# An encoder trunk on one core: the first outputs of a head two projections ahead of the second

## The chip, the cores and the metric

The kernel runs on one core of one Trainium2 chip. The metric is the time of one execution on the device in microseconds (us); lower is better. The time of the kernel before is the median of three runs.

## The reference, cut to what matters

One layer is applied to a prompt (1024 tokens) and to a sample (512 tokens), width 1024, all in float32. The token mixer that matters here is a gated linear recurrence with 8 heads of width 128 that runs forwards and backwards:

```
proj = rmsnorm(x) @ w_in                 # q, f_fw, f_bw, i, z_a, ... , g_a, g_b: 11 blocks of 1024
f = lb + (1 - lb) * sigmoid(f_raw);  k = (1 - lb) * sigmoid(-f_raw);  v = i
S_t = diag(f_t) S_{t-1} + k_t v_t^T;  o_t = S_t^T q_t      # forwards, and the same backwards
o = o_forward + o_backward
o = o * rsqrt(mean(o * o) + eps) * hnorm_g                 # per head
p_a = (o * silu(z_a)) @ w_a
```

A second branch (a short convolution with gates), the merge of both branches, one more projection and a last norm follow.

## The kernel before, in words

The program runs in stages. First the prompt's tokens are normed and projected (values, then all other blocks of the prompt, by a Strassen-like scheme that writes them to memory). Then comes the stage that the change touches: the recurrence of all 8 heads for prompt and sample, interleaved with the plain projections of the sample. After it the output projections follow.

In this stage each head has three blocks of 512 tokens: the prompt's blocks 0 and 1 (together one group) and the sample's one block (a group of its own). A block has four chunks of 128 tokens. The loop over `order` makes one turn for each block, 24 and one more, and a turn works on several blocks at once, in a software pipeline:

- `near_scores(prev)` (L450) and `scores(prev)` (L463): small products of 32 or 64 columns (L447, L481) of the decayed keys and queries, into the banks `sc`; ScalarE and VectorE copy them together into the tile `pt`.
- `transpose_keys(prev)` (L490) and `contributions(prev)` (L501): the keys are transposed (L496) and multiplied with the values (L509), and ScalarE copies the products to `us` (L510).
- `decays(cur)` (L409): for the next block, seven levels of decayed keys and queries, on VectorE (`K` L433, `Q` L413 and L434), ScalarE (copies into `cat`, L431 and L432) and GpSimd (products of the forget gates `T`, L421).
- `states(g)` (L513): when all blocks of a group are done, a chain of VectorE operations over the chunks turns the contributions into states, in place in `us` (L518): 12 for a prompt group, 4 for a sample group.
- `outputs(g, b)` (L521): for one block of a group, the products of scores with values and of queries with states (L533: 11 for a prompt block, 10 for a sample block; the trace counts each of these float32 products twice, as 22 and 20), all into the single bank `o`. Then ScalarE squares them and reads the sums (L537, four pairs), VectorE adds eps (L538), GpSimd raises to the power -1/2 (L98), and ScalarE copies the scaled products to the tile `oz` (L541, four). Only then is the bank free.
- `finish(g)` (L543): transposes of `oz` for all blocks of a group (L547), a product with the gate (L548), a store.
- `unit()`: one projection of the sample, 24 products of 512 columns (L94; 96 for the two wide ones, L87). Three units a turn. Their weights are loaded and split (L63 on ScalarE, L64 on VectorE) three units ahead.

Since a prompt group is complete after its block 1, the turns of a head differ. In the turn whose `prev` is the sample block (turn 1 below), `to_output` is the prompt group and nothing is to be finished. In the next turn (turn 2; `prev` is block 0 of the next head) `to_output` is the sample group, which has one block only, so its second `outputs` call finds no block, and `to_finish` is the prompt group. In turn 3 (`prev` is block 1) nothing is to be output, and the sample group is finished.

What sets the order: TensorE executes in the order in which the program is written (a manual schedule, L381). All other engines, and the queue of transfers, get their order from a planner, which simulates the program and prefers what stands earlier in it; once planned, each engine works strictly in that order. Buffers that matter: bank `o` one, banks `u` two, `sc` two, the projections' `pp` three (eight in all); `Q`, `K`, `F`, `pt` and `oz` three tiles each, `cat` eight, `us` and the values one for each kind of group.

The body of `outputs` after its products, for one block:

```python
                for c in range(CPB):
                    A.activation(oz[:, c, :], p[:, c, :], AF.Square, accum_out=ss[:, c:c + 1])
                V.tensor_scalar(ss, ss, 1.0 / P, EPS, op0=ALU.mult, op1=ALU.add)
                r = rsqrt(gp, ss, "o")
                for c in range(CPB):
                    A.activation(oz[:, c, :], p[:, c, :], AF.Copy, scale=r[:, c:c + 1])
```

The loop itself stands whole in the section on the change. After the loop come `unit()`, `outputs` of the last sample group, `finish`, `unit()` and `finish`; these stay as they are.

Of the kernel before, what the change touches and what calls it, by code (L numbers as in the profile page):

```python
# [43 lines left out]
def trunk_kernel(ctx: ExitStack, tc: tile.TileContext, xs, w, outs, masks_d, ident_d):  # L44
# [51 lines left out]
    def rsqrt(pool, t, name):  # L96
        r = pool.tile(list(t.shape), F32, name=f"rs_{name}")
        G.tensor_tensor(r, t, neghalf[:, :t.shape[-1]], op=ALU.pow)  # L98
        return r
# [275 lines left out]
    with outer:  # L375
# [7 lines left out]
        def gtile(name, shape, bufs=1):  # L383
            return gp.tile([P, *shape], F32, name=name, bufs=bufs)

        def bank(name, bufs, shape=(CPB, P)):
            return ps.tile([P, *shape], F32, name=name, bufs=bufs)
# [12 lines left out]
        def loaded(group, b):  # L400

            k = Block(group, b)
            src = fkq_d[k.tb][group.h]
            load(k.F, src[:, 0:2, :])
            load(k.K, src[:, 2:4, :])
            load(k.q, src[:, 4, :])
            return k

        def decays(k):  # L409

            F, K, q = k.F, k.K, k.q
            k.Q = Q = gtile("Q", [2, TB], 3)
            V.scalar_tensor_tensor(Q, ap(q, 0, [[0, 2], [1, TB]]), float(P) ** -0.5, F, op0=ALU.mult, op1=ALU.mult)  # L413
            k.kd = gtile("kd", [TB], 2)
            V.tensor_tensor(k.kd, K[:, 0, :], K[:, 1, :], op=ALU.add)

            Ts = [(F, TB)]
            while Ts[-1][1] > CPB:
                t, m = Ts[-1]
                tn = gtile(f"T{TB * 2 // m}", [2, m // 2], 1 if m // 2 > CPB else 4)  # L420
                G.tensor_tensor(tn, ap(t, 0, [[m, 2], [2, m // 2]]), ap(t, 1, [[m, 2], [2, m // 2]]), op=ALU.mult)  # L421
                Ts.append((tn, m // 2))
            k.total = Ts[-1][0]
            k.cats = []
            for hs, (t, m) in zip(LEVELS, Ts):
                nb = TB // (2 * hs)
                cat = gtile("cat", [2, TB], 8)
                k.cats.append(cat)
                kall = ap(K, TB, [[2 * hs, nb], [hs - TB, 2], [1, hs]])
                qall = ap(Q, 0, [[2 * hs, nb], [hs + TB, 2], [1, hs]])  # L430
                A.copy(ap(cat, 0, [[2 * hs, nb], [hs, 2], [1, hs]]), kall)  # L431
                A.copy(ap(cat, TB, [[2 * hs, nb], [hs, 2], [1, hs]]), qall)  # L432
                V.tensor_tensor(kall, kall, ap(t, m + 1, [[2, nb], [-m - 1, 2], [0, hs]]), op=ALU.mult)  # L433
                V.tensor_tensor(qall, qall, ap(t, 1, [[2, nb], [m - 1, 2], [0, hs]]), op=ALU.mult)  # L434
# [15 lines left out]
        def near_scores(k):  # L450

            k.sc = []
            score_products(k, range(4))
            k.near = near = gtile("near", [CPB, Q32])
            A.activation(near, k.sc[0][:, 0, :, :], AF.Copy, scale=float(P) ** -0.5)
            for li in range(1, 4):
                pick(k, li)
# [5 lines left out]
        def scores(k):  # L463

            score_products(k, range(4, 7))
            for li in range(4, 6):
                pick(k, li)
            k.pt = pt = gtile("pt", [CPB, P], 3)
            for s in range(4):
                r, x = slice(s * Q32, (s + 1) * Q32), slice((s ^ 1) * Q32, ((s ^ 1) + 1) * Q32)  # L470
                A.copy(pt[r, :, x], k.sc[1][r, 2, :, :])
                A.copy(pt[r, :, r], k.near[r, :, :])
            far_scores(k)
# [11 lines left out]
        def chunks_for(k, d):  # L485

            cs = [c for c in range(CPB) if (k.b * CPB + c < k.g.n - 1 if d else k.b * CPB + c > 0)]
            return cs, slice(cs[0], cs[-1] + 1)

        def transpose_keys(k):  # L490
            k.kT = []
            for d in (1, 0):
                cs, span = chunks_for(k, d)
                p = bank("u", 2)
                for c in cs:
                    T.transpose(p[:, c, :], k.K[:, d, c * P:(c + 1) * P], ident)  # L496
                kT = gtile("kT", [CPB, P], 2)
                A.copy(kT[:, span, :], p[:, span, :])
                k.kT.append(kT)
# [13 lines left out]
        def states(g):  # L513
            us = g.us
            for d, cs in ((1, range(1, g.n - 1)), (0, range(g.n - 2, 0, -1))):
                for c in cs:
                    t = g.done[c // CPB].total[:, d, c % CPB:c % CPB + 1]
                    V.scalar_tensor_tensor(us[:, d, c, :], us[:, d, c + (1 - 2 * d), :], t, us[:, d, c, :],  # L518
                                           op0=ALU.mult, op1=ALU.add)

        def outputs(g, b):  # L521
            for k in g.done[b:b + 1]:
                p = bank("o", 1)
                for c in range(CPB):
                    n = k.b * CPB + c
                    cols = slice(c * P, (c + 1) * P)
                    mms = [(k.pt[:, c, :], g.v[:, n, :])]
                    if n > 0:
                        mms.append((k.Q[:, 1, cols], g.us[:, 1, n - 1, :]))
                    if n < g.n - 1:  # L530
                        mms.append((k.Q[:, 0, cols], g.us[:, 0, n + 1, :]))
                    for m, (l, r) in enumerate(mms):
                        T.matmul(p[:, c, :], l, r, start=m == 0, stop=m == len(mms) - 1)  # L533
                k.oz = oz = gtile("oz", [CPB, P], 3)
                ss = gtile("sso", [CPB], 2)
# [7 lines that stand above are left out]
        def finish(g):  # L543
            for k in g.done:
                p = bank("u", 2)
                for c in range(CPB):
                    T.transpose(p[:, c, :], k.oz[:, c, :], ident)  # L547
                V.tensor_tensor(k.oz, p, g.zg[:, k.b * TB:(k.b + 1) * TB].rearrange("p (c t) -> p c t", c=CPB), op=ALU.mult)  # L548
                store(oz_d[k.tb][g.h], k.oz.rearrange("p c t -> p (c t)"))
# [84 lines left out]
        def prepare(n):  # L634
            while todo and len(ready) < n:
                p, m = todo.pop(0)
                ready.append((m, p()))

        def unit():
            prepare(AHEAD + 1)  # L640
            if ready:
                m, x = ready.pop(0)
                m(x)
# [4 lines left out]
        def values(g):  # L648
            g.v = gtile(f"v{g.n}", [g.n, P])
            src = v_d[0:8] if g.n == 8 else v_d[8:12]  # L650
            load(g.v, src[:, :, g.h * P:(g.h + 1) * P].rearrange("c p e -> p c e"))
# [9 lines left out]
        prev, to_output, to_finish = None, None, None  # L661
        for i in range(len(order) + 1):
            cur = None
            if i < len(order):
                cur = nxt if order[i][0] else sample[order[i][1]]
                if i + 1 < len(order) and order[i + 1][0]:
                    nxt = loaded(*order[i + 1])
            if prev:
                near_scores(prev)
                transpose_keys(prev)  # L670
            if cur:
                decays(cur)
                if cur.b == 0:
                    values(cur.g)
                    if cur.g.n == 8:
                        cur.g.zg = gtile("zgp", [2 * TB])
                        load(cur.g.zg, zg_d[cur.g.h])
            unit()
            if prev:
                scores(prev)  # L680
                contributions(prev)
            if to_output:
                outputs(to_output, 0)
            unit()
            if to_output:
                outputs(to_output, 1)
            if to_finish:
                finish(to_finish)
            unit()
            to_finish, to_output = to_output, None  # L690
            if prev and len(prev.g.done) == len(prev.g.tbs):
                to_output = prev.g
                states(prev.g)
            prev = cur
# [280 lines left out]
```

## Time and profile before

| what | value |
| --- | --- |
| three runs | 1972.35, 1977.19, 1985.93 us; median 1977.19 |
| the profiled execution | 1982.88 us |
| its span, first to last instruction | 1981.1 us |
| mean granted clock of TensorE | 0.988 of 2.4 GHz |
| busy: TensorE, VectorE, ScalarE, GpSimd | 1940.3, 1476.4, 981.5, 170.2 us |
| stage of the recurrence, in the span | about 900 to 1580 us |

The profile holds one execution. Times in it count from the span's start. A timeline row gives the start, the duration, the engine, the line of the program, the operation, what it writes and reads, how many instructions are merged, and in brackets how long the engine sat idle before it and what it waited for. Matmuls are pipelined: the next starts before the modelled end of the one before, so lengths of a stretch of TensorE's work are best taken from start to start.

### The profile page before, as it was taken

How to read it: one execution, taken by the hardware profiler on the slowest of the kernel's cores; microseconds unless marked ns; L12 is line 12 of the kernel's file. 1: busy time of each engine (PE TensorE's matmuls, PEld its weight loads, DVE VectorE, ACT ScalarE, POOL GpSimd, SP SyncE). 2: the span in 40 equal slices, each digit the busy share in tenths (PEclk: the TensorE clock that was granted, in tenths of full speed). 3: DMA queues.
4: the chain of work that ended last, by engine and by line, in shares of the span. 5: the costliest groups of instructions: out<-in, count | busy, mean ns of one | idle time of the engine just before them, and what ended most of it. 6: DMA issues, size and time to landing. Idle time of an engine off the chain costs nothing.

```text
span 1981.1 us, 37160 instructions
## 1 busy us (share of the span) xinstructions
PE 1940.3 (98%) x14820; PEld 1633.4 (82%) x14820; DVE 1476.4 (75%) x2369; ACT 981.5 (50%) x1956; POOL 170.2 (9%) x220
## 2 busy tenths in 40 slices
PE   9999999999999999998999999999999999999998
PEld 8988888888888888886888888888888887888786
DVE  6558686878676777776688878879788378765687
ACT  6433333343424333345677877877877443332332
POOL 1000000000000000003121322322212000000000
PEclk8999999999999999998999999999999999999999
DMA  7433333333324242435443534434333497798653
GB/s 214 146 108 103 115 96 107 102 120 97 120 88 131 77 138 75 128 113 184 146 124 118 161 112 128 142 106 156 110 120 104 143 308 254 241 313 278 214 186 107
DMA packets 313757, 288.85 MB, mean 146 GB/s; under 512 B 19184, under 2 KB 252912, under 8 KB 313584
## 3 DMA queue, kind: packets, MB, share of 16 engines
q1 hardware_dynamic: 313584, 286.49, 45.8%
q8 instruction: 116, 1.90, 0.4%
q14 instruction: 57, 0.47, 0.1%
HBM read 208.84 MB, written 77.59 MB: 145 GB/s over the span
## 4 chain that ended last, share of the span: by engine, by line
PE 77%; issue 9%; DVE 5%; DMA 5%; ACT 3%; POOL 1%; SPq 0%; DVEq 0%; POOLq 0%; ACTq 0%
PE pp L309 38%; PE pp L94 16%; PE pw L781 9%; PE pp L215 5%; PE o L533 2%; PE pp L87 2%; PE sc L447 2%; DMA io<-in_w_o 1%; PE u L509 1%; DVE Q L434 1%; DVE K L433 1%; ACT cat L431 1%; DVE w_l L64 1%; DMA w_raw<-in_w_b 1%; PE tp L177 1%
## 5 line engine op out<-in xcount | busy, mean ns | idle before, releaser
L309 PE MATMUL pp<-s_h,w_h 128*128 128x512 f32 x1120 | 435.9, 389 | 1.2 <-ACT w_h L63 1.2
L309 PE MATMUL pp<-s_l,w_h 128*128 128x512 f32 x1120 | 435.7, 389 | 0.0
L309 PE MATMUL pp<-s_h,w_l 128*128 128x512 f32 x1120 | 435.7, 389 | 0.0
L63 ACT ACTIVATE w_h<-w_raw 128x1024 fp32r<-128x1024 f32 (+1 forms) x250 | 209.6, 838 | 323.4 <-PE pp L309 137.8
L94 PE MATMUL pp<-s_h,w_h 128*128 128x512 f32 x896 | 356.5, 398 | 0.0
L94 PE MATMUL pp<-s_h,w_l 128*128 128x512 f32 x896 | 350.0, 391 | 1.5 <-DVE w_l L64 1.5
L94 PE MATMUL pp<-s_l,w_h 128*128 128x512 f32 x896 | 350.0, 391 | 0.2 <-DVE s_l L64 0.2
L64 DVE TENSOR_TENSOR w_l<-w_raw,w_h 128x1024 fp32r<-128x1024 f32 (+1 forms) x250 | 238.4, 954 | 101.0 <-ACT w_h L63 99.4
L314 DVE TENSOR_TENSOR tmp<-pp,tmp 128x512 f32<-128x512 f32 x240 | 165.3, 689 | 156.1 <-PE pp L309 156.1
L309 PEld LDWEIGHTS pp<-s_h,w_h 128*128 128x128 f32 x1120 | 210.2, 188 | 45.3 <-ACT w_h L63 1.8
L309 PEld LDWEIGHTS pp<-s_l,w_h 128*128 128x128 f32 x1120 | 210.2, 188 | 43.6
L309 PEld LDWEIGHTS pp<-s_h,w_l 128*128 128x128 f32 x1120 | 210.2, 188 | 43.6
L63 ACT ACTIVATE w_h<-w_S 128x512 fp32r<-128x512 f32 x160 | 101.0, 632 | 263.4 <-PE pp L309 263.3
L94 PEld LDWEIGHTS pp<-s_h,w_l 128*128 128x128 f32 x896 | 168.6, 188 | 38.3 <-DVE w_l L64 2.3
L94 PEld LDWEIGHTS pp<-s_l,w_h 128*128 128x128 f32 x896 | 168.9, 189 | 34.1 <-DVE s_l L64 1.0
L94 PEld LDWEIGHTS pp<-s_h,w_h 128*128 128x128 f32 x896 | 169.2, 189 | 33.0 <-ACT w_h L63 0.3
L431 ACT COPY cat<-K 128x512 f32<-128x512 f32 x168 | 111.6, 668 | 36.8 <-DVE K L433 35.4
L433 DVE TENSOR_TENSOR K<-K,T 128x512 f32<-128x512 f32 x144 | 110.1, 764 | 18.7 <-ACT cat L431 17.4
L432 ACT COPY cat<-Q 128x512 f32<-128x512 f32 x168 | 111.4, 668 | 19.4 <-DVE Q L434 10.8
L434 DVE TENSOR_TENSOR Q<-Q,T 128x512 f32<-128x512 f32 x144 | 104.0, 722 | 16.2 <-ACT cat L432 15.5
L781 PE MATMUL pw<-s_h,w_h 128*128 128x512 f32 x280 | 110.6, 395 | 2.5 <-ACT w_h L63 2.5
L781 PE MATMUL pw<-s_h,w_l 128*128 128x512 f32 x280 | 110.5, 395 | 1.1 <-DVE w_l L64 1.1
(178 smaller groups left out, 2961.5 us busy)
## 6 DMA issues: line engine op xcount, KB each, us to landing
w_raw<-in_w_in SPq DMA_DIRECT2D x166, 512.0 KB, 4.4
fkq_d<-sg SPq DMA_DIRECT2D x48, 256.0 KB, 2.3
io<-cz_p SPq DMA_DIRECT2D x20, 512.0 KB, 5.4
fkq_d<-sk SPq DMA_DIRECT2D x32, 256.0 KB, 2.1
F<-fkq_d SPq DMA_DIRECT2D x16, 512.0 KB, 3.7
K<-fkq_d SPq DMA_DIRECT2D x16, 512.0 KB, 6.5
w_raw<-in_w_b SPq DMA_DIRECT2D x16, 512.0 KB, 4.8
w_raw<-in_w_a SPq DMA_DIRECT2D x16, 512.0 KB, 6.1
```

Source lines behind the costliest of these rows:

```text
L63: A.activation(hi, src, AF.Copy)
L64: V.tensor_tensor(lo, src, hi.bitcast(F32), op=ALU.subtract)
L87: T.matmul(out, lhs(k, a), parts[k // 2][b][:, k % 2, :], start=k == 0 and n == 0, stop=k == KT - 1 and n == 2)
L94: T.matmul(out, whl[a][:, k, :], rhs(k, b), start=k == 0 and n == 0, stop=k == KT - 1 and n == 2)
L215: T.matmul(pp, B[f"B{k // 4 + 1}{t + 1}"][a][:, k % 4, c * P:(c + 1) * P], parts[k][b], start=k == 0 and m == 0, stop=k == KT - 1 and m == 2)
L309: T.matmul(bank, hl[x][:, k, :], B[b][y][:, k, :], start=k == 0 and i == 0, stop=k == 3 and i == 2)
L314: V.tensor_tensor(out, p, t, op=ALU.add)
L431: A.copy(ap(cat, 0, [[2 * hs, nb], [hs, 2], [1, hs]]), kall)
L432: A.copy(ap(cat, TB, [[2 * hs, nb], [hs, 2], [1, hs]]), qall)
L433: V.tensor_tensor(kall, kall, ap(t, m + 1, [[2, nb], [-m - 1, 2], [0, hs]]), op=ALU.mult)
L434: V.tensor_tensor(qall, qall, ap(t, 1, [[2, nb], [m - 1, 2], [0, hs]]), op=ALU.mult)
L781: T.matmul(bank, hl[x][:, c:c + P], O[n][y][:, k, :], start=k == 0 and i == 0, stop=k == 3 and i == 2)
```

## The change

`outputs(to_output, 0)` moves from behind `contributions(prev)` to a place directly behind `transpose_keys(prev)`, ahead of `decays(cur)` and of the first of the turn's three units. `finish(to_finish)` changes places with `outputs(to_output, 1)`. Nothing else changes. The loop with the diff:

```diff
         for i in range(len(order) + 1):
             cur = None
             if i < len(order):
                 cur = nxt if order[i][0] else sample[order[i][1]]
                 if i + 1 < len(order) and order[i + 1][0]:
                     nxt = loaded(*order[i + 1])
             if prev:
                 near_scores(prev)
                 transpose_keys(prev)
+            if to_output:
+                outputs(to_output, 0)
             if cur:
                 decays(cur)
                 if cur.b == 0:
                     values(cur.g)
                     if cur.g.n == 8:
                         cur.g.zg = gtile("zgp", [2 * TB])
                         load(cur.g.zg, zg_d[cur.g.h])
             unit()
             if prev:
                 scores(prev)
                 contributions(prev)
-            if to_output:
-                outputs(to_output, 0)
             unit()
+            if to_finish:
+                finish(to_finish)
             if to_output:
                 outputs(to_output, 1)
-            if to_finish:
-                finish(to_finish)
             unit()
             to_finish, to_output = to_output, None
             if prev and len(prev.g.done) == len(prev.g.tbs):
                 to_output = prev.g
                 states(prev.g)
             prev = cur
```

## Rows read from the trace of the kernel before

**Rows 1.** Table of engines of the page: busy us, share of span, instructions.

```profile
PE 1940.3 (98%) x14820; PEld 1633.4 (82%) x14820; DVE 1476.4 (75%) x2369; ACT 981.5 (50%) x1956; POOL 170.2 (9%) x220
```

**Rows 2.** Busy time by stretch (busy us and instructions of each engine), 1200 to 1300 us.

```profile
1200.00:1300.00 100.00, 97.99 (x1417) 82.87 (x1416) 86.50 (x145) 78.55 (x179) 25.39 (x32) 1.00 0.45 138
```

**Rows 3.** Waits of TensorE, 900 to 1580 us: total us, times, longest.

```profile
PE o L533 <- ACT oz L541: 14.1, 7, 2.1
PE u L496 <- DVE K L433: 4.8, 1, 4.8
```

**Rows 4.** Timeline of TensorE, turn 1 of the second head.

```profile
1072.17 0.48 PE L94 MATMUL pp<-s_h,w_h 128*128 128x512 f32 x1
...
1080.89 0.39 PE L533 MATMUL o<-v,pt 128*128 128x128 f32 x2
...
1083.27 0.48 PE L94 MATMUL pp<-s_h,w_h 128*128 128x512 f32 x1
...
1090.94 0.49 PE L533 MATMUL o<-v,pt 128*128 128x128 f32 x2 [1.94 <-ACT oz L541]
...
1094.47 0.77 PE L94 MATMUL pp<-s_h,w_h 128*128 128x512 f32 x1
...
1100.68 0.46 PE L447 MATMUL sc<-q,kd 128*32 128x32 f32 x32
```

**Rows 5.** Timeline of ScalarE, turn 1 of the second head; last row: the fourth.

```profile
1074.86 0.62 ACT L431 COPY cat<-K 128x512 f32<-128x512 f32 x1 [1.45 <-DVE K L433]
...
1085.80 0.27 ACT L537 ACTIVATE oz<-o 128x128 f32<-128x128 f32 x1
...
1089.75 1.14 ACT L541 ACTIVATE oz<-o,rs_o 128x128 f32<-128x128 f32 x4 [0.43 <-POOL rs_o L98]
...
1255.17 1.14 ACT L541 ACTIVATE oz<-o,rs_o 128x128 f32<-128x128 f32 x4 [1.88 <-POOL rs_o L98]
```

**Rows 6.** Timeline of TensorE, turn 1 of the fourth and of the last head.

```profile
1239.68 0.48 PE L94 MATMUL pp<-s_h,w_h 128*128 128x512 f32 x1
...
1247.40 0.49 PE L533 MATMUL o<-v,pt 128*128 128x128 f32 x2 [2.01 <-ACT oz L541]
...
1249.88 0.47 PE L94 MATMUL pp<-s_h,w_h 128*128 128x512 f32 x1
...
1255.54 0.46 PE L447 MATMUL sc<-q,kd 128*32 128x32 f32 x32
...
1257.56 0.48 PE L94 MATMUL pp<-s_h,w_h 128*128 128x512 f32 x1
...
1548.63 0.48 PE L94 MATMUL pp<-s_h,w_h 128*128 128x512 f32 x1
...
1554.19 0.38 PE L533 MATMUL o<-v,pt 128*128 128x128 f32 x2
```

**Rows 7.** Stretches of 10 us; the third number from the end is the granted clock.

```profile
1010.00:1020.00 10.00, 7.92 (x40) 6.93 (x39) 7.08 (x13) 7.03 (x20) 3.97 (x6) 0.83 0.32 100
...
1240.00:1250.00 10.00, 7.99 (x47) 6.73 (x46) 6.84 (x10) 8.53 (x25) 2.66 (x3) 1.00 0.17 52
...
1400.00:1410.00 10.00, 8.36 (x41) 7.53 (x42) 7.50 (x11) 6.59 (x21) 5.10 (x7) 0.83 0.55 157
...
1550.00:1560.00 10.00, 10.00 (x57) 8.67 (x56) 1.77 (x4) 4.65 (x20) 2.01 (x2) 1.00 0.26 80
```

**Rows 8.** Timeline of VectorE, second head.

```profile
1068.79 1.13 DVE L518 SCALAR_TENSOR_TENSOR us<-us,T 128x128 f32<-128x128 f32 x3
...
1077.03 0.69 DVE L433 TENSOR_TENSOR K<-K,T 128x512 f32<-128x512 f32 x1 [0.76 <-ACT cat L431]
...
1083.73 1.22 DVE L413 SCALAR_TENSOR_TENSOR Q<-q,F 128x1024 f32<-128x1024 f32 x1
```

**Rows 9.** Timeline of GpSimd, turn 1 of the second head: the two powers.

```profile
1088.71 1.01 POOL L98 TENSOR_TENSOR rs_o<-sso,neghalf 128x4 f32<-128x4 f32 x1 [24.88 <-DVE sso L538]
...
1097.05 1.91 POOL L98 TENSOR_TENSOR rs_o<-sso,neghalf 128x4 f32<-128x4 f32 x1
```

## The prediction

> **What bounds the kernel now.** I read the table of engines first: TensorE is busy for 98% of the span [rows 1], and in the stage of small products a stretch of 100 us shows it at 98.0 while VectorE stands at 86.5 and ScalarE at 78.6 [rows 2]. So TensorE's own stream sets the time, and a change is worth what it takes out of that stream's gaps. The waits of TensorE in this stage come next [rows 3]. Almost all of them have one form: the products of `outputs` (L533) wait for the scaling copies of ScalarE (L541), 7 times, 14.1 us in total, never over 2.1 us. The only other wait of any size comes once, at the start of the stage, and the change does not touch it.
>
> The timeline of TensorE in the second head shows which `outputs` waits [rows 4]. In turn 1, block 0's products start at 1080.89, one projection starts at 1083.27, and block 1's products start only at 1090.94, after 1.94 us of idle. There is one bank `o`. Block 1 may not write it before ScalarE has read block 0 out of it twice, with VectorE's small operation and GpSimd's power between, and one projection is too short a cover. The ScalarE rows of the same turn show the chain: block 0's squares begin at 1085.80, more than 2 us after the products ended, because copies of the scores stand before them in ScalarE's queue, and the last scaling copy ends at 1089.75 + 1.14 = 1090.89, 0.05 before the products of block 1 [rows 5].
>
> **The stall, and what follows it.** A projection without a wait behind it takes 1554.19 - 1548.63 = 5.56 us from its start to that of the products; that is the last head, where no decays compete and no idle stands [rows 6]. In the second head it takes 1090.94 - 1083.27 = 7.67 [rows 4], in the fourth 1247.40 - 1239.68 = 7.72 [rows 6]. One stall so costs 2.11 to 2.16 us, and seven at 2.16 are 15.1 us. (The 14.1 of rows 3 count idle from modelled ends, which lie a little late.)
>
> Second, the clock. Around the stalls the stretches of 10 us show a mean granted clock of 0.83, the first at 1010 to 1020 and the last at 1400 to 1410, five such in all; at the other two stalls it stays at 1.00, as at 1240 to 1250 [rows 7]. So the clock falls to its lower level (1.2 instead of 2.4 GHz) for a while after five of seven stalls, and nowhere else from 1000 to 1580. Its price, by rows: in the fourth head, at full clock, block 1's products and the projection behind them take 1255.54 - 1247.40 = 8.14 us [rows 6]; in the second they take 1100.68 - 1090.94 = 9.74 [rows 4]. That is 1.60 us, times five is 8.0 us.
>
> Here a rule can be weighed. The Trainium skill, "TensorE: Matmul & The Clock Gate", section "Why this matters for your kernels", advises against idle gaps of TensorE that are clearly longer than these 2 us, as what brings the lower clock. Rows 7 with rows 3 disagree as far as they go: five falls, each directly behind one of these gaps. By the page's advice the falls would have another cause and would stay, and the sum would hold the stalls alone, 15.1 us.
>
> **The change part by part.** *The outputs of block 0 go ahead.* No instruction is added or removed. In turn 1, block 0's 22 products move from behind `contributions` to a place directly behind the key transposes, so two projections and two groups of small products lie between block 0 and block 1 instead of one projection. Block 0's chain needs 7.67 us from the end of its products to the free bank [rows 4]. The new cover is at least the two projections, 2 x 5.56 = 11.1 us. The stall of block 1 goes whole.
>
> What the moved products now need earlier: the states of the prompt head (L518), block 0's copied scores, Q, and the bank. The last three state operations start at 1068.79 and take 1.13 us, so they end at 1069.92 [rows 8]; the products' new place is where the projection starts now, 1072.17 [rows 4]. The margin is 2.25 us where it was 10.97 us. The margin is there, and the states stand before turn 1's work in program order, so I take 0 as the cost. The bounds: nothing if the order of VectorE stays; if the last three state operations fall behind the work that VectorE does next, up to the K operation that ends at 1077.03 + 0.69 = 1077.72, the wait is 1077.72 - 1072.17 = 5.6 us a head.
>
> What is queued behind the moved work on the other engines: ScalarE gets the four squares, four accumulator reads and four scaling copies while it has holes (in the second head it waits 1.45 us before the copy of K at 1074.86 [rows 5]). Behind them stand cat copies of the next block and the splits of weights, which are prepared three projections ahead. GpSimd is idle for 24.88 us before block 0's power now [rows 9], so the power finds it free earlier. No DMA moves with `outputs`; the stores belong to `finish`.
>
> A gain without a direct price: the first operation on the next block's Q starts at 1083.73 [rows 8], directly after block 0's products [rows 4], since Q has three buffers and block 0's products free one. Freed 8.7 us earlier, the Q chain can spread over the projections; TensorE does not wait for it now, so I book 0.
>
> *The sample's outputs* (one block) move in turn 2 in the same way, and this is where the bank wait could go next: block 1's products, then one projection, then the near scores and transposes, then these. From the projection's start to the new place are 1257.56 - 1249.88 = 7.68 us [rows 6]. Block 1's chain in this head ends at 1255.17 + 1.14 = 1256.31 [rows 5], 1.25 us in time. Even if it took as long as block 0's chain, 7.67 us, it would just do. So again 0. Nothing can be won below that, since no wait stands there now [rows 3]; as the bound above I take a whole GpSimd power in its slower form, 1.91 us [rows 9], seven times 13.4 us.
>
> *`finish` ahead of the second `outputs`.* In turn 1 nothing waits to be finished (the turn before has no outputs), and in turn 2 the sample group has no second block, so `outputs(…, 1)` issues nothing. The two calls never both issue work in one turn; exchanging them changes nothing, cost 0.
>
> *The last head* has no stall now [rows 6], so it gives nothing.
>
> The sum: 15.1 + 8.0 = 23.1 us. The profiled execution took 1982.88 us for a span of 1981.1; it would take 1959.8. It is 5.7 us above the median of the runs shown, 1977.19, and I have no reason to scale the gain, so the forecast for the median is 1977.2 - 23.1 = 1954.1 us.
>
> **The rivals.**
>
> (a) The bank wait moves to the sample's outputs. For it: the margin is 1.25 us in the fourth head [rows 5, 6], the order of ScalarE will be planned anew, and the second of two powers is the slow one (1.91) [rows 9]. Against: with Q done earlier ScalarE has less to do at that point. A wait of 1.5 us a head gives back 10.5: 1964.6.
>
> (b) The clock falls stay, for another cause than the gaps: only 15.1 is won, 1962.1. Against: the last head has no gap at block 1's products, and the clock stays at 1.00 there, 1550 to 1560 [rows 6, 7]. (The page named above would have it so.)
>
> (c) VectorE or ScalarE becomes the bound. Block 1's products start at 1090.94 in the second head and at 1247.40 in the fourth [rows 4, 6], so a head takes 78.2 us; VectorE works 86.5% of it [rows 2], and shortened by 3.3 us it would work 90%. Against: one engine at 90% with room in its queue still keeps up. If it gives back two thirds: 1969.5.
>
> (d) Slower: the states come late. In turn 1 VectorE's queue is written out by the planner; if the last state operations are placed behind the next block's first K operations, TensorE waits 5.6 us a head right behind the transposes [rows 8]; seven are 39 us, and the falls of the clock stay: 1977.2 - 15.1 + 39 = 2001. It decides for slower once the states are later by 2.25 us of margin and about 2.2 more. Against: in program order the states stand before all of turn 1's work, and their last operations ran before the next block's K [rows 8].
>
> **How the numbers follow.** The forecast 0.62, (a) 0.18, (b) 0.08, (c) 0.06, (d) 0.06. A measurement of this kernel can tell about 1% from no change, here 19.8 us. The forecast's own range is 1948 to 1961: between three and seven falls of the clock (4.8 to 11.2 us in place of 8.0) and some 4 us for the median of three runs that lie 13.6 us apart. Some of it, and (a), (b) and (c), fall short of 1%. Faster by over 1%: 0.57; within: 0.37; slower: 0.06. The range of 1945 to 1968 leaves out (d), most of (c) and the tails.
>
> **What would show it.** Right: no wait of L533 for L541 in TensorE's waits; granted clock 1.00 from 1000 on; in turn 1 the order transposes, products, projection; Q's first operation some 8 us earlier against the near scores. Step by step wrong: a wait of L533 for L518 (d), a wait of L533 for L541 in turn 2 (a), 0.83 without a gap before it (b), waits of projections for the splits L63 or L64, or of scores for the cat copies (c). A median above 1968 or below 1945 makes the prediction wrong.

## The result, and the profile after

The changed kernel takes 1957.64 us (median of 4 runs, 1954.35 to 1960.89); the kernel before 1977.63 (4 runs). The ratio is 0.9895 with a 95% interval of 0.9871 to 0.9919, so 20.0 us by the medians, and 16 to 25.5 by the interval. The forecast was 1954.1 with a gain of 23.1; range and sign hold, and the gain lies inside the interval. The profiled execution took 1960.89 us against 1982.88.

The waits of TensorE in the stage, as in [rows 3]:

```profile
PE u L496 <- DVE K L433: 4.3, 1, 4.3
PE o L533 <- ACT oz L541: 1.8, 3, 1.0
PE pp L87 <- DVE w_l L64: 1.3, 1, 1.3
PE pp L87 <- ACT w_h L63: 1.3, 1, 1.3
PE o L533 <- DVE us L518: 1.3, 1, 1.3
```

The row that carried 14.1 us in 7 waits holds 1.8 in 3, and these stand at another place, as will be seen. A wait for the states (L518) has come in, once.

Turn 1 and the start of turn 2 of the second head on TensorE, beside [rows 4]:

```profile
1071.57 0.39 PE L533 MATMUL o<-v,pt 128*128 128x128 f32 x2
...
1073.94 0.48 PE L94 MATMUL pp<-s_h,w_h 128*128 128x512 f32 x1
...
1082.57 0.47 PE L94 MATMUL pp<-s_h,w_h 128*128 128x512 f32 x1
...
1088.13 0.38 PE L533 MATMUL o<-v,pt 128*128 128x128 f32 x2
...
1096.17 0.46 PE L447 MATMUL sc<-q,kd 128*32 128x32 f32 x32
...
1098.44 0.49 PE L533 MATMUL o<-v,pt 128*128 128x128 f32 x2
```

Block 0's products start at 1071.57, two projections follow, and block 1's products start 5.56 us after the second projection (1082.57 to 1088.13), which is the undisturbed distance of [rows 6], not the 7.67 of [rows 4]. From there to the near scores it takes 8.04 us, at full clock, where it took 9.74. The last row is the sample's outputs in their new place.

The clock by stretches of 50 us (third number from the end), to be held against [rows 7]:

```profile
1000.00:1050.00 50.00, 48.99 (x713) 41.57 (x713) 42.17 (x68) 42.94 (x109) 15.12 (x17) 1.00 0.39 120
1050.00:1100.00 50.00, 49.99 (x723) 42.58 (x722) 43.12 (x74) 37.76 (x91) 11.71 (x16) 1.00 0.46 139
...
1400.00:1450.00 50.00, 50.00 (x711) 42.27 (x710) 46.34 (x79) 37.95 (x90) 14.31 (x16) 1.00 0.46 142
```

It stays at 1.00 in all eleven stretches from 1000 to 1550 us; none of the five falls is left, and TensorE is busy for 48.99 to 50.00 of 50. The first operation on the next block's Q, on VectorE, starts at 1074.71, 21.5 us before the near scores; before the change it was 17.0 us (1083.73 to 1100.68), with the stall and the slow clock inside.

### The profile page after: what moved, and what is told of

Read it like the earlier page. It is cut to its first block, busy times and chain, and to the rows that moved or that the text cites. A ratio compares the mean times of both kernels' runs of the same rounds, so it can differ in the third digit from the quotient of the medians.

```text
span 1959.1 us, 37141 instructions
## 1 busy us (share of the span) xinstructions
PE 1928.7 (98%) x14820; PEld 1624.1 (83%) x14820; DVE 1476.6 (75%) x2369; ACT 976.3 (50%) x1956; POOL 173.8 (9%) x220
## 4 chain that ended last, share of the span: by engine, by line
PE 83%; DMA 5%; DVE 4%; ACT 3%; issue 3%; POOL 1%; SPq 0%; DVEq 0%; POOLq 0%; ACTq 0%
PE pp L309 39%; PE pp L94 20%; PE pw L781 9%; PE pp L215 5%; PE o L533 2%; PE pp L87 2%; PE sc L447 2%; PE u L509 2%; DMA w_raw<-in_w_in 1%; DVE w_l L64 1%; DVE Q L434 1%; ACT cat L432 1%; PE u L496 1%; DMA io<-sgb_s 1%; ACT cat L431 1%
## 5 line engine op out<-in xcount | busy, mean ns | idle before, releaser
L434 DVE TENSOR_TENSOR Q<-Q,T 128x512 f32<-128x512 f32 x144 | 117.6, 817 | 12.4 <-ACT cat L432 10.6
L432 ACT COPY cat<-Q 128x512 f32<-128x512 f32 x168 | 112.5, 670 | 27.6 <-DVE Q L434 13.9
L421 POOL TENSOR_TENSOR T<-F 128x512 f32<-128x512 f32 x24 | 36.2, 1508 | 983.5 <-DMA F<-fkq_d 848.8
L431 ACT COPY cat<-K 128x512 f32<-128x512 f32 x168 | 111.8, 670 | 23.1 <-DVE K L433 21.3
L64 DVE TENSOR_TENSOR w_l<-w_S,w_h 128x512 fp32r<-128x512 f32 x160 | 109.2, 684 | 2.0 <-ACT w_h L63 2.0
```

The costliest lines, as they stand in the source:

```text
L64: V.tensor_tensor(lo, src, hi.bitcast(F32), op=ALU.subtract)
```

## The experiments

Each run is told with its median and its ratio to runs of the kernel before on the same chip. In the diffs `+` and `-` are against the kernel named.

**Where the two parts of the move pay.** The first call of `outputs` moves for prompt groups (8 chunks) and for sample groups (4 chunks). Two kernels move one of them alone. Against the changed kernel, the first is:

```diff
-            if to_output:
+            if to_output and to_output.n == 8:
                 outputs(to_output, 0)
...
                 contributions(prev)
+            if to_output and to_output.n == 4:
+                outputs(to_output, 0)
             unit()
```

> Only the prompt groups' block 0 goes ahead; the sample's outputs stay behind contributions. Theory (the single bank o, with the clock falls as its consequence, is the whole gain): no wait of block 1's products for L541, clock 1.00 from 1000 to 1560 us, and the three small bank waits of the sample's outputs (1.8 us in the changed kernel) go too: 1953 to 1958 us, 1 to 3 us under the changed kernel's 1957.6. Rival (the moved sample outputs carry part of the gain, for instance by freeing the sample's Q earlier): slower than the changed kernel by 3 us or more, about 1962.

Measured: 1956.43 us, ratio 0.988 (0.9858 to 0.9902). No wait of L533 is left at all; the first three rows of TensorE's waits are

```profile
PE u L496 <- DVE K L433: 4.4, 1, 4.4
PE pp L87 <- DVE w_l L64: 1.3, 1, 1.3
```

and the third is 0.5 us. The theory holds: the prompt's block 0 carries the whole gain. That this kernel is faster than the changed one is not shown; the intervals overlap by more than half their length.

The second has the numbers 8 and 4 exchanged.

> Only the sample's outputs go ahead; the prompt's block 0 stays behind contributions. Theory: the 7 stalls of about 2 us and the falls of the clock behind them stay: 1975 to 1980 us, as before. If the sample's products now come before block 1's bank is free, some 1 to 2 us a head more. Rival (the sample's move carries part of the gain): 1970 or less.

Measured: 1981.7 us, ratio 1.001 (0.9997 to 1.0024).

```profile
PE o L533 <- ACT oz L541: 14.7, 7, 2.6
```

The seven stalls are there as before, with four falls of the clock in the stage, and the ratio cannot be told from 1 (the time itself is 1.7 us above the expected range). The sample's move alone is worth nothing.

**`finish` alone.** Against the kernel before only the two calls change places.

> Only finish and the second outputs change places; the prompt's and the sample's first outputs stay. Theory: in no turn do both issue work, so the same instructions run in the same order: ratio to the kernel before 1.000 within its interval; what differs from 1 is the noise of this measurement.

Measured: 1981.96 us, ratio 1.0007 (0.9995 to 1.002), and the lists of instructions of all engines and of the transfers are the same as before, row by row. This exchange is empty. It also shows the noise: the same program, 2 us by the medians. Its profiled execution has six falls of the clock where that of [rows 7] has five.

**Is it the bank?** The kernel before with two banks `o`, paid for by one of the projections' three banks; and a control that only gives that bank away.

```diff
-                p = bank("o", 1)
+                p = bank("o", 2)
...
-                pp = ps_p.tile([P, TB], F32, name="pp", bufs=3)
+                pp = ps_p.tile([P, TB], F32, name="pp", bufs=2)
```

The second change is made in all three places where the projections ask for a bank; the control has it alone.

> The order of before, with two banks o, and two instead of three banks for the projections (there are eight in all). Theory (the single bank is what block 1 waits for): no wait of L533 for L541 and no fall of the clock from 1000 to 1560 us; against the control with two projection banks and one bank o it is 18 to 24 us faster. Rival (the wait is for ScalarE's or TensorE's own order): the stalls stay, no difference to the control.

> The control for the two banks o: the order of before, one bank o, two banks for the projections. Both theories: the 7 stalls and most falls of the clock as before; what two projection banks cost is the difference to before, expected 0 to 15 us.

Measured: 1966.18 us (0.9931, 0.9914 to 0.9948) with two banks `o`, 1983.51 (1.0013, 1.0004 to 1.0023) for the control: 17.3 us. The control's waits first, then those with two banks `o`:

```profile
PE o L533 <- ACT oz L541: 14.1, 7, 2.1
```

```profile
PE sc L481 <- DVE near L460: 9.7, 8, 3.1
```

Without touching the order of TensorE the stall is gone; so it was the one bank. One fall of the clock is left in the stage where the control has six. But the gain is 17 us, short of the 18 to 24 expected, and a wait has taken the stall's place that was not there before: the far scores (L481) wait for VectorE's picks of the near scores (L460) to free a bank `sc`.

**Do the gaps bring the falls of the clock?** The kernel before, with nine products of 512 columns put into the gap. Their results are used by nothing.

```diff
             unit()
+            if to_output and to_output.n == 8 and cur:
+                fill = ps_p.tile([P, TB], F32, name="pp", bufs=3)
+                for _ in range(9):
+                    T.matmul(fill, hT[0][0][:, 0, 0:P], hT[0][0][:, 0, :], start=True, stop=True)
             if to_output:
                 outputs(to_output, 1)
```

> The order of before, with nine more products of 512 columns (some 2.0 us of TensorE at full clock, their results unused) between the projection and block 1's products in the seven heads that stall. Theory (the gaps bring the falls of the clock): the bank is free no earlier, but the falls from 1000 to 1560 us are gone, so 6 to 10 us faster than before: 1967 to 1972. Rival (the falls have another cause and stay): granted clock 0.83 in the same places, 1975 to 1982.

Measured: 1973.81 us, ratio 0.9975 (0.9963 to 0.9987), that is 5 us (2.6 to 7.3) by the ratio and 6.3 by the medians. The timeline of TensorE in the second head:

```profile
1084.68 0.48 PE L94 MATMUL pp<-s_h,w_h 128*128 128x512 f32 x1
...
1090.23 2.20 PE L688 MATMUL pp<-s_h 128*128 128x512 f32 x9
1092.40 0.49 PE L533 MATMUL o<-v,pt 128*128 128x128 f32 x2
```

and the stretches of 50 us around two of the places where the clock had fallen:

```profile
1050.00:1100.00 50.00, 50.00 (x659) 42.43 (x650) 42.33 (x74) 37.28 (x89) 8.93 (x13) 1.00 0.47 141
...
1400.00:1450.00 50.00, 50.00 (x713) 42.32 (x713) 45.80 (x76) 40.79 (x98) 16.20 (x21) 1.00 0.50 149
```

From the projection's start to block 1's products it takes 7.72 us, as in [rows 4, 6]: the filling frees the bank no earlier. But TensorE is not idle, and the clock stays at 1.00 in all stretches from 1000 to 1550. Added work makes the kernel faster. So the gaps brought the falls. The time misses the expected 1967 to 1972: by the medians the falls cost 5 to 6 us where 8.0 were worked out, and 8.0 lies just outside the interval. The section on why the prediction was right sets this kernel's stage beside the others.

**How far ahead is enough?** Against the changed kernel, both first outputs go back by one projection:

```diff
                 transpose_keys(prev)
-            if to_output:
-                outputs(to_output, 0)
             if cur:
...
             unit()
+            if to_output:
+                outputs(to_output, 0)
             if prev:
                 scores(prev)
```

> Both first outputs stand behind the turn's first projection, ahead of scores, so one projection and two groups of small products (8.6 us) lie between the prompt's two blocks instead of two projections and them. Theory (block 0's chain lasted 7.7 us only because copies of scores stood before it on ScalarE): the stall goes whole or to under 0.5 us a head, the one wait for the states in the first head goes, and so do the sample's small waits: 1953 to 1959 us. Rival (two projections are needed as cover): stalls of 1 us or more a head stay, with some falls of the clock: 1964 to 1972.

Measured: 2019.91 us, ratio 1.02 (1.0178 to 1.0222). Neither the theory nor the rival: 40 us slower than before, and hardly by the stall. A new wait stands in the list, and behind each of the seven the clock falls (granted clock 0.66 to 0.76 in stretches of 10 us).

```profile
PE u L547 <- ACT us L510: 48.9, 7, 7.5
...
PE o L533 <- ACT oz L541: 0.3, 1, 0.3
```

In turn 2 `finish` waits 7 us for banks `u`, which ScalarE's copies of the contributions (L510) have to free. ScalarE's timeline and TensorE's in the second head:

```profile
1117.60 0.27 ACT L537 ACTIVATE oz<-o 128x128 f32<-128x128 f32 x1
...
1123.84 0.63 ACT L541 ACTIVATE oz<-o,rs_o 128x128 f32<-128x128 f32 x2 [1.23 <-POOL rs_o L98]
...
1125.39 0.63 ACT L541 ACTIVATE oz<-o,rs_o 128x128 f32<-128x128 f32 x2
...
1128.49 0.97 ACT L510 COPY us<-u 128x512 f32<-128x512 f32 x2
```

```profile
1129.13 1.97 PE L547 MATMUL u<-ident,oz 128*128 128x128 f32 x8 [6.91 <-ACT us L510]
```

The sample's squares and scaling copies, from 1117.60 on, stand before the copies of the scores and of the contributions in ScalarE's queue, and hold them up until 1128.49. To see which of the two moves does this, each was put behind the first projection alone; the other stayed where it does no harm.

> The prompt's block 0 stands as in the change, the sample's outputs behind turn 2's first projection, ahead of scores. Theory (there they push ScalarE's copies of the contributions behind them, and finish waits for the banks u): the waits of L547 for L510 are back, 40 to 50 us in 7 times, with falls of the clock: 2010 to 2025 us. Rival (the prompt's place made those waits): no such waits, 1953 to 1960.

Measured: 1998.76 us, ratio 1.0099 (1.0081 to 1.0117).

```profile
PE u L547 <- ACT us L510: 27.0, 7, 4.7
```

The mechanism is the sample's outputs at that place, again with seven falls of the clock, but the size missed: 27 us of waits and not 40 to 50, 1998.76 us and not 2010 to 2025. In the second head the sample's squares start 1.0 us after the modelled end of their products here, 4.2 us after it in the run with both moved back. So the prompt's place adds to what ScalarE has queued ahead of them; what exactly was not taken apart.

> The prompt's block 0 stands behind the turn's first projection, the sample's outputs stay behind contributions. Theory (the 49 us of waits in the run with both behind the first projection come from the sample's outputs in turn 2, and one projection with two groups of small products covers block 0's chain): no wait of finish for L510, stalls of block 1 under 0.5 us a head, 1953 to 1959 us, like the run with only the prompt ahead. Rival (one projection is too short a cover for the prompt, too): waits of L533 for L541 of 1 us or more a head, 1962 to 1975.

Measured: 1967.46 us, ratio 0.9943 (0.9927 to 0.996). The stall is gone (0.3 us in all) and no fall of the clock is left in the stage, so one projection and two groups of small products do cover block 0's chain. Yet it is 10 us slower than the changed kernel, by the same wait as with two banks `o`:

```profile
PE sc L481 <- DVE near L460: 12.6, 8, 2.7
```

VectorE and TensorE at one such wait, in turn 2:

```profile
1101.80 1.16 DVE L434 TENSOR_TENSOR Q<-Q,F 128x512 f32<-128x512 f32 x1 [2.85 <-ACT cat L432]
...
1105.09 0.30 DVE L460 COPY_PREDICATED near<-mk,sc 128x128 f32<-128x128 uint8 x1
```

```profile
1107.13 0.69 PE L481 MATMUL sc<-cat 128*64 128x64 f32 x16 [1.56 <-DVE near L460]
```

The picks stand behind an operation on Q (L434, the first level of the block that follows the next one), which waited 2.85 us for ScalarE's copy L432. ScalarE and GpSimd show why that copy is late:

```profile
1099.88 1.15 ACT L541 ACTIVATE oz<-o,rs_o 128x128 f32<-128x128 f32 x4 [2.90 <-POOL rs_o L98]
1100.89 0.87 ACT L432 COPY cat<-Q 128x512 f32<-128x512 f32 x1
```

```profile
1095.43 3.44 POOL L421 TENSOR_TENSOR T<-T 128x16 f32<-128x16 f32 x2 [1.38 <-DVE Q L434]
1098.84 1.00 POOL L98 TENSOR_TENSOR rs_o<-sso,neghalf 128x4 f32<-128x4 f32 x1
```

It stands behind the scaling copies of the prompt's block 1, these wait for the power, and the power stands behind GpSimd's last products of the gates T, which had waited for VectorE's work on the next block's Q. In the changed kernel these products start at 1089.31 and take 0.50 us instead of 3.44 (why is not shown), GpSimd is idle for 6.39 us before the power at 1096.20, and L432 runs at 1096.07, ahead of the scaling copies.

The next block's Q starts at 1080.4 here, 16.5 us before its near scores; in the changed kernel at 1074.7, 21.5 us before them. So the trace leads from the later Q over GpSimd and ScalarE to the picks, and suggests that the second projection of lead buys time for Q, not for the bank. A fourth buffer for Q was to test it, in this kernel and in the kernel before, paid for by the second buffer of `kd` and by small constants that move to a pool of the first stage (left out of the diff):

```diff
-            k.Q = Q = gtile("Q", [2, TB], 3)
+            k.Q = Q = gtile("Q", [2, TB], 4)
...
-            k.kd = gtile("kd", [TB], 2)
+            k.kd = gtile("kd", [TB], 1)
```

> The prompt's block 0 behind the turn's first projection and the sample's outputs in their old place, as in the run that ended at 1967.5 us, with a fourth buffer for Q (paid for by one buffer of kd and by small constants put elsewhere). Theory (that run lost 10 to 13 us in the waits of L481 for L460 because block 0's products free Q one projection later, so the next block's Q work is late on VectorE in turn 2): with a free buffer Q's first operation starts before block 0's products, the waits of L481 fall under 3 us, 1954 to 1960 us. Rival (those waits come from the order of VectorE around the moved products, whatever Q's buffers): the waits stay at 10 us or more, 1964 to 1971.

> The order of before with the fourth buffer for Q (and one of kd) alone. Theory (the bank o sets the stall, not Q): the seven waits of L533 for L541 stay, 10 to 15 us, with falls of the clock: 1972 to 1982 us. Rival (freeing Q early is itself the gain): 1965 or less.

Measured: 1997.38 us (1.0093, 1.0072 to 1.0115) and 2022.3 us (1.0222, 1.0199 to 1.0244). Both miss. In the first Q does start before block 0's products and the waits of L481 are gone, as the theory had it, but others stand in their place:

```profile
PE o L533 <- ACT oz L541: 10.2, 7, 2.1
PE u L496 <- DVE K L433: 4.3, 1, 4.3
PE u L496 <- DVE oz L548: 3.4, 6, 0.6
```

In the second the price of the fourth buffer shows in VectorE's own waits:

```profile
DVE kd L415 <- PE sc L447: 33.0, 7, 5.1
```

With one `kd` VectorE stands still until the near scores are read, 4.7 us a head, and the seven waits of L533 for L541 come to 28.4 us instead of 10 to 15. Moreover, in both runs the stage starts 22 to 23 us later than in the kernel before, by work that Q has no part in. From 200 to 300 us, the kernel before first, then the second of these runs:

```profile
200.00:300.00 100.00, 100.00 (x443) 82.81 (x442) 73.25 (x120) 36.04 (x61) 0.00 (x0) 1.00 0.33 104
200.00:300.00 100.00, 100.00 (x430) 80.17 (x429) 73.83 (x120) 35.09 (x59) 0.00 (x0) 1.00 0.33 103
```

At full clock and without idle time TensorE gets 430 products done where it got 443. Of the edit only the moved constants reach that far ahead; how they do this is open. The pair is spoilt by what paid for it and decides nothing about Q. It stays open whether the late Q alone makes the waits of L481 or the order that the planner gives VectorE around the moved products.

**The changed kernel again,** beside the two runs that put one of the moves back by a projection.

> The changed kernel itself once more, beside the others on one chip. Both theories: 1954 to 1961 us, some 20 to 24 us under the kernel before; whether its three small bank waits of the sample's outputs and the one wait for the states are there in another execution (2 to 4 us in all), and so whether the run with only the prompt ahead can be told from it.

Measured: 1957.32 us, ratio 0.9893 (0.9877 to 0.9909).

```profile
PE o L533 <- ACT oz L541: 0.3, 1, 0.3
```

The wait for the states is not there, and of the sample's bank waits 0.3 us is left. The 3.1 us of small waits in the first profile are not in every execution of the program.

## Why the prediction was right

The stage can be compared between profiled executions, from the start of turn 1's key transposes in the first head to the start of the last transposes of `finish`:

| kernel | from | to | us |
| --- | --- | --- | --- |
| before | 993.53 | 1576.15 | 582.62 |
| before, gap filled | 995.87 | 1570.19 | 574.32 |
| changed | 993.98 | 1556.35 | 562.37 |
| changed, again | 992.85 | 1552.00 | 559.15 |

*The stall.* Right in mechanism and size: it needed the single bank (two banks remove it), all of it lay in the prompt's block 1, and block 1's products now start 5.56 us after the projection before them. 15.1 us were booked. Between the filled gap, where the stall is whole and no fall is left, and the second run of the changed kernel lie 15.17 us.

*The clock.* The cause was right, and shown: with the gap filled, the falls go though the stall stays. In the stage this took off 8.30 us for the five falls of this execution, where 8.0 were booked. How many falls an execution has is the less certain part: the profiles with seven idle gaps of 2 us show four to six. The Trainium skill, "TensorE: Matmul & The Clock Gate", section "Why this matters for your kernels", advises against gaps clearly longer than these; it does not say that shorter ones are harmless, and gaps of 2.0 us were enough here.

*The sum.* The stage became 20.25 us shorter, and with the 3.1 us of new waits that is 23.3; in the second run, where these waits are nearly gone, it is 23.47 shorter. 23.1 were booked. These are single executions.

*The margins.* The wait for the states was booked at 0 with 2.25 us of margin in the second head; it held there and failed once, by 1.25 us, in the first head of one execution. There the margin had been only 0.55 us: the kernel before, where the projection starts at 994.16, shows

```profile
992.49 1.12 DVE L518 SCALAR_TENSOR_TENSOR us<-us,T 128x128 f32<-128x128 f32 x3
```

The prediction read the second head alone. The sample's bank was booked at 0 with 1.25 us of margin, by the chain as it stood; this is the step that was off. The third head after the change, VectorE, then ScalarE, then TensorE:

```profile
1168.62 0.51 DVE L147 TENSOR_SCALAR F<-F,om_lbf,lbf 128x512 f32<-128x512 f32 x1
...
1169.77 1.22 DVE L413 SCALAR_TENSOR_TENSOR Q<-q,F 128x1024 f32<-128x1024 f32 x1
1170.91 0.17 DVE L538 TENSOR_SCALAR sso<-sso 128x4 f32<-128x4 f32 x1
```

```profile
1167.31 0.58 ACT L145 ACTIVATE F<-pp 128x512 f32<-128x512 f32 x1
...
1168.27 0.27 ACT L537 ACTIVATE oz<-o 128x128 f32<-128x128 f32 x1
...
1169.02 0.29 ACT L537 ACTIVATE oz<-o 128x128 f32<-128x128 f32 x1
...
1172.19 1.14 ACT L541 ACTIVATE oz<-o,rs_o 128x128 f32<-128x128 f32 x4 [0.30 <-POOL rs_o L98]
```

```profile
1164.87 0.47 PE L94 MATMUL pp<-s_h,w_h 128*128 128x512 f32 x1
...
1173.39 0.49 PE L533 MATMUL o<-v,pt 128*128 128x128 f32 x2 [0.59 <-ACT oz L541]
```

From the start of the projection behind block 1's products the chain takes 1173.33 - 1164.87 = 8.46 us; in the fourth head before it took 1256.31 - 1249.88 = 6.43 [rows 5, 6]. The greater part of this arises on ScalarE, which the prediction held to have less to do at that point: there the squares started at once (1250.17), while now ScalarE comes late, and the copies of the forget gates (L145, L146) still stand before them. The last square ends 4.44 us after that start, where it ended after 2.50 (at 1252.38). On VectorE the next Q operation (1.22 us) stands before the small operation on which the power waits; that adds 1.1 us. The power gives back 0.9, since it takes 1.01 us instead of 1.91. So the margin is used up. Rival (a) came in so far, with 1.8 us in one execution and 0.3 in another.

*`finish`* was worth nothing, as worked out. *Rivals (b), (c)* and *(d)* did not come; but the run with both outputs one projection later shows a stronger form of the other side than (d): 40 us lost by a place that looks harmless on TensorE's list.

*Q.* "A gain without a direct price" was booked at 0, because TensorE did not wait for it. Against the kernel before that is right. But without the stall and with Q freed one projection later, 12.6 us of waits appear that the stall had covered. One projection of lead is enough for the bank, but the kernel is 10 us slower than with two; that Q is the reason is what the trace suggests and no run decides.

By the medians the gain is 20.0 and 20.3 us against 23.1, which lies inside both intervals. The profiled execution that the prediction was worked out from is one of the slower ones (1982.88 us against a median of 1977.63); its mean granted clock is 0.988, that of 21 other executions of this kernel, beside the filled gap, 0.988 to 0.993 with a median of 0.990. So it probably had more falls than most, and the 8.0 us were booked from it.

## What to carry to other kernels

Between two uses of a single accumulator bank TensorE needs other work that lasts as long as the whole chain that reads the bank out, on every engine in it. Moving the first use earlier removes the wait without a second bank. But the moved group then also stands at another place in the in-order queues of the other engines: here both moves one projection later cost 40 us, twice the gain. After a stall is taken out, look for the waits that it covered, and check a margin in every head, not in one. A gap of TensorE of 2 us cost 1.6 to 1.7 us more through the clock where the clock fell.

## What was not expected of the hardware

Gaps of 2.0 us on TensorE were enough for falls of the clock, and nine useless products put into each made the kernel 5 us faster. The same gap brought a fall in some heads and none in others, four to six of seven by execution. With the prompt's block 0 behind the first projection, a gap of 2.7 us and six of 1.6 to 1.7 us brought none. And in the two runs with a fourth buffer for Q, a hundred us of dense products ahead of the stage held 430 instead of 443 at the same granted clock of 1.00, which no run explains.
